# Squared-ReLU MLP: first layer by one level of Strassen's method (Winograd's form), MLP in 4 chunks

## The chip, the cores and the metric

The kernel runs on one core of a Trainium2 chip. The metric is the device time of one execution in microseconds (us); the figure quoted for a kernel is the median of several executions. Engines are named as in the profile: PE is TensorE, PEld its weight loads, DVE is VectorE, ACT is ScalarE, POOL is GpSimd, SP issues most DMA.

## What is computed

One layer of a streaming encoder on 512 tokens (S) of width 1024 (D):

```
h = rmsnorm(x); [u|v|bg|cg|xs|ga|gb] = h @ w_in          # 1024 x 7168
a = gelu(u) * (blockwise spatial gating of rmsnorm(gelu(v)))
c = bg * causal_conv3(cg * xs)
m = sigmoid(ga) * (a @ w_proj_a) + sigmoid(gb) * (c @ w_proj_b)
x = x + m @ w_out
z = relu(rmsnorm(x) @ w_ff1)                             # 1024 x 4096
x = x + (z * z) @ w_ff2                                  # 4096 x 1024
y = rmsnorm(x)
```

All data is float32. The change is to the two MLP products (the last three lines but one), and to the weight stream that all of the products share.

## The kernel before

Channels lie on the 128 partitions and tokens on the free axis. Every float32 operand is split into hi + lo, both in the type float32r, and a product is three TensorE matmuls: hi*hi, hi*lo, lo*hi (lines 120 to 122).

The weight stream comes in **units** of 1024 x 128 weights (512 KB). `prep` (line 97) loads a unit into a `raw` tile (4 of them) through SP's queue, rounds it to `whi` on ACT (line 84) and subtracts to get `wlo` on DVE (line 85); `wsp` holds 3 pairs of whi and wlo, and preparation runs two units ahead. `unit_matmuls` (line 110) then issues 8 k tiles x 3 = 24 matmuls of 128 x 128 weights on 512 tokens into one PSUM bank.

The MLP runs in 2 chunks (`NCH = 2`), each with 16 tiles of 128 of the 4096 inner channels. In a chunk the first layer takes 16 units; each bank goes through `z_evac` (line 365): max(.,0) times the token's rstd on DVE (`t_z`, line 367), the square on ACT (`q`, line 369), and a split into zh and zl (lines 84, 85). Then for each of the 8 output tiles the second layer takes two units (48 matmuls into one bank), and DVE adds the bank to `res` (line 475). The norm's statistic for the first layer (`rstd_of`, `spread`) is worked out while the first two tiles run. The very last output tile (`last_tile`, line 409) is done by halves of 256 tokens, in 96 matmuls of 256 columns (lines 424 to 426), so that the final norm of the first half runs beside the second.

Each engine works in the order of its own instruction list, which the tile framework's scheduler writes; an instruction that waits holds up what is behind it on its engine.

Of the kernel before, what the change touches and what calls it, by code (L numbers as in the profile page):

```python
# [31 lines left out]
def hybrid_block(ctx, tc, xT, vecs, w_v, w_main, w_s, b_s, out_a, out_b):  # L32
# [12 lines left out]
    outp = ctx.enter_context(tc.tile_pool(name="outp", bufs=4))  # L45
# [19 lines left out]
    # TensorE reaches its full clock while the first loads are under way.  # L65
# [15 lines left out]
    def split_into(hi, lo, src, scale=None):  # L81
        """hi + lo = src (or src * scale), each part rounded to float32r."""
# [12 lines left out]
    parts = {}  # L95

    def prep(i):
        if i >= n_units or i in parts:
            return
        r = raws.tile([P, KT * P], F32, name="raw")  # L100
        nc.sync.dma_start(r, w_main[i])
        hi = wsp.tile([P, KT * P], F32R, name="whi")
        lo = wsp.tile([P, KT * P], F32R, name="wlo")
        split_into(hi, lo, r)
        parts[i] = (hi, lo)

    state = {"next": 0}
    AHEAD = 2

    def unit_matmuls(psum, act_hi, act_lo, start=True, stop=True, cols=slice(0, S)):  # L110
        """psum += W_unit.T @ act over the unit's 8 k tiles."""
        i = state["next"]
        state["next"] += 1
        prep(i)
        for a in range(1, AHEAD + 1):
            prep(i + a)
        hi, lo = parts.pop(i)
        for k in range(KT):
            ks = slice(k * P, (k + 1) * P)
            nc.tensor.matmul(psum, hi[:, ks], act_hi[k][:, cols], start=start and k == 0, stop=False)  # L120
            nc.tensor.matmul(psum, hi[:, ks], act_lo[k][:, cols], start=False, stop=False)  # L121
            nc.tensor.matmul(psum, lo[:, ks], act_hi[k][:, cols], start=False, stop=stop and k == KT - 1)  # L122
# [23 lines left out]
    def spread(r, n=NB):  # L146
        """rstd as [token, block] -> [any partition, token], in PSUM."""
# [10 lines left out]
    xh = [shared("X", 16, f"xh{k}", F32R) for k in range(KT)]  # L158
    xl = [shared("X", 16, f"xl{k}", F32R) for k in range(KT)]
    acc = shared("acc", 1, "acc")  # L160
    vt = [[shared("V", 8, f"vt{b}{h}") for h in range(2)] for b in range(NB)]
    wsT = [shared("M", 16, f"wsT{i}").rearrange("p (g i) -> p g i", i=P) for i in range(2)]
    bsb = [shared("M", 16, f"bsb{i}").rearrange("p (g i) -> p g i", i=P) for i in range(2)]
    vsum = small.tile([P, 2, NB], F32, name="vsum")

    vparts = {}

    def prep_v(i):
        if i >= 2 * KT:
            prep(i - 2 * KT)  # L170
# [4 lines left out]
        t = raws.tile([P, KT * P], F32, name="raw")[:, :HALF]  # L175
        nc.sync.dma_start(t, w_v[h, k])
        vh = shared("M", 16, f"vh{h}{k}", F32R)
        vl = shared("M", 16, f"vl{h}{k}", F32R)
# [30 lines left out]
    for i in range(2 * KT):  # L209
# [330 lines left out]
```

## Time and profile before

| | |
|---|---|
| median of 3 executions | 813.45 us (813.43 to 813.47) |
| profiled execution, first to last instruction (span) | 811.9 us |
| PE busy | 804.2 us (99%), 3646 matmuls |
| PEld busy | 667.2 us (82%) |
| DVE busy | 376.0 us (46%) |
| ACT busy | 250.6 us (31%) |
| DMA | 81.35 MB, mean 100 GB/s |

The profile gives the span of the profiled execution and no other time of it; the median of the timed runs lies 1.55 us above that span. The share of busy time is an average over stages, and a busy PE is not a PE at its peak, since matmuls overlap in the records: how fast it works is read from the starts of successive matmuls. An engine's idle time counts only where another waits for it.

### The profile page before, as it was taken

Reading aid. Unit: us, or ns where it says so; the run is one execution under the profiler, and the core shown is the slowest. Engines: PE = TensorE matmul, PEld = TensorE weight load, DVE = VectorE, ACT = ScalarE, POOL = GpSimd, SP = SyncE. Lnnn points to the kernel's source line nnn. Section 1 sums busy time; section 2 is a strip of 40 time slices with the busy share of each in tenths; the row PEclk is TensorE's granted clock in tenths of the full one; section 3 lists DMA queues with packets and bytes.
Section 4 is the critical chain, followed back from the end, with each engine's and each line's share of the span. In section 5 each row is a group of like instructions: output and inputs, shape, how many; then the busy total and the mean of one; then the engine's idle time right before and its main releaser. Section 6 shows DMA issues by size and latency. Waiting matters only on the chain.

```text
span 811.9 us, 8874 instructions
## 1 busy us (share of the span) xinstructions
PE 804.2 (99%) x3646; PEld 667.2 (82%) x3646; DVE 376.0 (46%) x501; ACT 250.6 (31%) x324; POOL 6.1 (1%) x15
## 2 busy tenths in 40 slices
PE   9999999999999999999999999999999999999996
PEld 6888888888888888888888888888888888888886
DVE  7555653334555555444455554442233445434433
ACT  7323332222212222332344253332112334422221
POOL 0000000000000000000000000000000000000000
PEclk9999999999999999999999999999999999999998
DMA  7522223322332233233223223223322332233203
GB/s 247 195 105 104 78 77 105 104 90 92 104 104 82 100 105 103 79 104 103 93 89 105 97 84 105 101 81 104 103 93 89 105 103 85 97 104 104 79 0 105
DMA packets 25352, 81.35 MB, mean 100 GB/s; under 512 B 2768, under 2 KB 3792, under 8 KB 25312
## 3 DMA queue, kind: packets, MB, share of 16 engines
q1 hardware_dynamic: 24416, 79.18, 29.1%
q10 hardware_dynamic: 864, 1.57, 0.6%
q8 instruction: 28, 0.46, 0.3%
q14 instruction: 12, 0.10, 0.0%
q0 software_dynamic: 32, 0.03, 0.0%
HBM read 78.68 MB, written 2.10 MB: 99 GB/s over the span
## 4 chain that ended last, share of the span: by engine, by line
PE 98%; DMA 0%; ACT 0%; DVEq 0%; POOLq 0%; POOL 0%; DVE 0%; issue 0%
PE bank L121 30%; PE bank L120 30%; PE bank L122 30%; PE bank L219 5%; PE bank L270 1%; PE bank L425 0%; PE bank L426 0%; PE bank L424 0%; DMA res<-xT 0%; PE bank L152 0%; PE st L141 0%; DVEq L534 0%; PE bank L393 0%; PE st L441 0%; POOLq L534 0%; ACT xh L87 0%
## 5 line engine op out<-in xcount | busy, mean ns | idle before, releaser
L84 ACT CAST whi<-raw 128x1024 fp32r<-128x1024 f32 x136 | 143.4, 1054 | 494.2 <-PE bank L121 373.9
L85 DVE TENSOR_TENSOR wlo<-raw,whi 128x1024 fp32r<-128x1024 f32 x136 | 166.5, 1225 | 78.7 <-ACT whi L84 77.6
L120 PE MATMUL bank<-xh,whi 128*128 128x512 f32 x384 | 150.0, 391 | 0.0
L121 PE MATMUL bank<-xl,whi 128*128 128x512 f32 x384 | 149.4, 389 | 0.0
L122 PE MATMUL bank<-xh,wlo 128*128 128x512 f32 x384 | 149.4, 389 | 0.0
L120 PE MATMUL bank<-x2h,whi 128*128 128x512 f32 x256 | 99.8, 390 | 0.0
L122 PE MATMUL bank<-x2h,wlo 128*128 128x512 f32 x256 | 99.6, 389 | 0.0
L121 PE MATMUL bank<-x2l,whi 128*128 128x512 f32 x256 | 99.6, 389 | 0.0
L120 PE MATMUL bank<-zh,whi 128*128 128x512 f32 x240 | 93.4, 389 | 0.0
L121 PE MATMUL bank<-zl,whi 128*128 128x512 f32 x240 | 93.4, 389 | 0.0
L122 PE MATMUL bank<-zh,wlo 128*128 128x512 f32 x240 | 93.4, 389 | 0.0
L122 PEld LDWEIGHTS bank<-xh,wlo 128*128 128x128 f32 x384 | 72.1, 188 | 15.0
L120 PEld LDWEIGHTS bank<-xh,whi 128*128 128x128 f32 x384 | 72.2, 188 | 14.8
L121 PEld LDWEIGHTS bank<-xl,whi 128*128 128x128 f32 x384 | 72.1, 188 | 14.6
L367 DVE SCALAR_TENSOR_TENSOR t_z<-bank,Rf 128x512 f32<-128x512 f32 x32 | 22.0, 691 | 78.8 <-PE bank L122 78.8
L121 PEld LDWEIGHTS bank<-x2l,whi 128*128 128x128 f32 x256 | 48.1, 188 | 10.0
L122 PEld LDWEIGHTS bank<-x2h,wlo 128*128 128x128 f32 x256 | 48.1, 188 | 10.0
L120 PEld LDWEIGHTS bank<-x2h,whi 128*128 128x128 f32 x256 | 48.1, 188 | 9.9
L121 PEld LDWEIGHTS bank<-zl,whi 128*128 128x128 f32 x240 | 45.1, 188 | 9.4
L122 PEld LDWEIGHTS bank<-zh,wlo 128*128 128x128 f32 x240 | 45.1, 188 | 9.3
L120 PEld LDWEIGHTS bank<-zh,whi 128*128 128x128 f32 x240 | 45.1, 188 | 9.3
L475 DVE TENSOR_TENSOR res<-bank,res 128x512 f32<-128x512 f32 x15 | 10.4, 692 | 50.1 <-PE bank L122 50.1
(118 smaller groups left out, 818.6 us busy)
## 6 DMA issues: line engine op xcount, KB each, us to landing
raw<-w_main SPq DMA_DIRECT2D x136, 512.0 KB, 3.2
raw<-w_v SPq DMA_DIRECT2D x16, 256.0 KB, 4.0
res<-xT SPq DMA_DIRECT2D x8, 256.5 KB, 4.8
out_a<-o SPq DMA_DIRECT2D x4, 256.0 KB, 2.4
wsT<-w_sT ACTq DMA_DIRECT2D x2, 256.0 KB, 5.0
bsb<-b_sb ACTq DMA_DIRECT2D x2, 256.0 KB, 5.5
out_b<-ob ACTq DMA_DIRECT2D x2, 256.0 KB, 3.0
out_b<-ob SPq DMA_DIRECT2D x2, 256.0 KB, 3.1
```

Source lines behind the costliest of these rows:

```text
L84: nc.scalar.copy(hi, src)
L85: nc.vector.tensor_tensor(lo, src, hi.bitcast(F32), op=ALU.subtract)
L120: nc.tensor.matmul(psum, hi[:, ks], act_hi[k][:, cols], start=start and k == 0, stop=False)
L121: nc.tensor.matmul(psum, hi[:, ks], act_lo[k][:, cols], start=False, stop=False)
L122: nc.tensor.matmul(psum, lo[:, ks], act_hi[k][:, cols], start=False, stop=stop and k == KT - 1)
L219: nc.tensor.matmul(vbanks[h][b], xs[k][:, b * P : (b + 1) * P], ws, start=k == 0 and ws is vh and xs is xh, stop=k == KT - 1 and xs is xl,)
L270: nc.tensor.matmul(pm[:, b * P : (b + 1) * P], vt[b][g // 4][:, (g % 4) * P : (g % 4 + 1) * P], wsT[g // 4][:, g % 4, :], start=True, stop ...
L367: nc.vector.scalar_tensor_tensor(t, pz, 0.0, Rf, op0=ALU.max, op1=ALU.mult)
L475: nc.vector.tensor_add(res[j], py, res[j])
```

## The change

**Strassen.** The first layer is computed for two output tiles (a **pair**, 256 inner channels) at a time, as a 2 x 2 block product: the 1024 x 256 weights are cut into four blocks of 512 x 128, and the activations into four of 512 x 256 (two halves of the channels by two halves of the tokens). Winograd's form of Strassen's method needs 7 block products (P1, P2, D, F, P6, E, P7) instead of 8; each is 4 k tiles x 3 = 12 matmuls of 256 columns. Left operands are weight blocks or sums of them, right operands activation blocks or sums of them.

- The activation sums are made once, by `combos`, while the output projection runs (its tiles are taken in the order 0, 4, 1, 5, ... so that the blocks that belong together are ready together).
- The weight sums are made per pair on DVE: `add1` (one instruction of 1024 elements per partition) and `add2` (two of 512). A pair then has four operands to split on ACT and DVE: t0 (two raw blocks), t1 (one raw block, 512 elements), t2 and t3 (two sums each).
- The products are gathered in three PSUM banks and put together on ACT (three copies of 256) and DVE (five instructions of 256) into the two output tiles c1 and c2, on which `z_evac` now works. P7 of a pair is issued behind P2 of the next pair (`flush_late`). P6 and P7 go on accumulating in the half bank A, after what stood there has been read.

**Chunks.** `NCH` is 4: 4 pairs, then 8 units of the second layer (24 matmuls each), four times; one pair of the next chunk is computed ahead (5, 4, 4 and 3 pairs). The last two output tiles instead of the last one are done by halves of the tokens, with 8 k tiles each.

**Weight stream.** `raw` tiles are 1 MB (two units, or a pair's four blocks), and there are 2. `whi`/`wlo` is a ring of 4 operands; an operand is prepared when the one four places before is done. v's weights have tiles of their own.

The core of the diff:

```diff
-NCH = 2
+NCH = 4
+RING = 4
-    raws = ctx.enter_context(tc.tile_pool(name="raws", bufs=4))
-    wsp = ctx.enter_context(tc.tile_pool(name="wsp", bufs=3))
+    raws = ctx.enter_context(tc.tile_pool(name="raws", bufs=2))
+    wsp = ctx.enter_context(tc.tile_pool(name="wsp", bufs=RING))
...
+            def add1(raw=raw, sm=sm):
+                nc.vector.tensor_tensor(
+                    sm[0], raw(1, 3), raw(3, 4).broadcast_to([P, 2, S]), op=ALU.add
+                )
+            def add2(raw=raw, sm=sm, key=key):
+                nc.vector.tensor_tensor(sm[1][:, 1, :], sm[0][:, 1, :], raw(1, 2)[:, 0, :], op=ALU.add)
+                nc.vector.tensor_tensor(sm[1][:, 0, :], sm[1][:, 1, :], raw(0, 1)[:, 0, :], op=ALU.add)
+                load_after(key)
+            tl = []
+            tl.append(add_operand(lambda raw=raw: raw(0, 2)))
+            steps.append((add1, None))
+            tl.append(add_operand(lambda raw=raw: raw(2, 3), n=1))
+            steps.append((add2, None))
+            tl.append(add_operand(lambda sm=sm: sm[1]))
+            tl.append(add_operand(lambda sm=sm: sm[0]))
...
+    LEFT = {"P1": (0, 1, "B11"), "P2": (0, 0, "B21"), "D": (1, 0, "nT4"), "F": (2, 0, "B22"),
+            "P6": (2, 1, "nT2"), "E": (3, 1, "nT1"), "P7": (3, 0, "T3")}
+    def product(p, name, out, first, last=False):
+        t, g, r = LEFT[name]
+        o = pairs[p][t]
+        pump()
+        need(o)
+        for sl in range(KS):
+            c = slice(sl * P, (sl + 1) * P)
+            w_hi, w_lo = o["hi"][:, g, c], o["lo"][:, g, c]
+            x_hi, x_lo = right[r, sl, 0], right[r, sl, 1]
+            nc.tensor.matmul(out, w_hi, x_hi, start=first and sl == 0, stop=False, skip_group_check=True)
+            nc.tensor.matmul(out, w_hi, x_lo, start=False, stop=False, skip_group_check=True)
+            nc.tensor.matmul(out, w_lo, x_hi, start=False, stop=sl == KS - 1, skip_group_check=True)
+        if name in ("P2", "D", "P6", "P7"):
+            o["done"] = True
...
+    def block_pair(p, after):
+        ba, bf, bd = bank(), bank(), bank()
+        A, P2 = ba[:, :N2], ba[:, N2:]
+        F = bf[:, :N2]
+        Dp, E = bd[:, :N2], bd[:, N2:]
+        c1, c2 = temp("c1"), temp("c2")
+        product(p, "P1", A, True)
+        product(p, "P2", P2, False)
+        nc.scalar.copy(c1[:, :N2], A)
+        nc.vector.tensor_add(c1[:, :N2], P2, c1[:, :N2])
+        flush_late()
+        product(p, "D", Dp, True)
+        product(p, "F", F, True)
+        product(p, "P6", A, False)
+        nc.scalar.copy(c1[:, N2:], A)
+        nc.vector.tensor_add(c1[:, N2:], F, c1[:, N2:])
+        product(p, "E", E, False)
+        def end():
+            product(p, "P7", A, False)
+            nc.vector.tensor_add(c1[:, N2:], E, c1[:, N2:])
+            nc.scalar.copy(c2[:, :N2], A)
+            nc.vector.scalar_tensor_tensor(c2[:, N2:], E, -1.0, c2[:, :N2], op0=ALU.mult, op1=ALU.subtract)
+            nc.vector.tensor_sub(c2[:, :N2], Dp, c2[:, :N2])
+            after(c1, c2)
+        late.append(end)
...
     for ck in range(NCH):
-        for i in range(CF):
-            pz = bank()
-            unit_matmuls(pz, xh2, xl2)
...
+        end = min((ck + 1) * CF // 2 + 1, NP1)
+        for p in range(done, end):
+            ff1_pair(p)
+        done = end
+        flush_late()
...
-                unit_matmuls(py, zh[0:8], zl[0:8], stop=False)
-                unit_matmuls(py, zh[8:16], zl[8:16], start=False)
+            unit_matmuls(py, zh, zl)
```

How the instruction lists change is shown at two places. The first is PE in the first layer. Before, a tile is 24 matmuls of 512 columns; these are the first six of the fourth tile (x2h, x2l are the activations' hi and lo):

```order
L120 MATMUL bank_3436<-x2h0_2961,whi_3348 128x512
L121 MATMUL bank_3436<-x2l0_2969,whi_3348 128x512
L122 MATMUL bank_3436<-x2h0_2961,wlo_3349 128x512
L120 MATMUL bank_3436<-x2h1_2962,whi_3348 128x512
L121 MATMUL bank_3436<-x2l1_2970,whi_3348 128x512
L122 MATMUL bank_3436<-x2h1_2962,wlo_3349 128x512
```

Now the same engine in the changed kernel, at the end of P2 of the third pair (bank_3448, operand 3393) and the start of the late P7 of the second pair (bank_3322, operand 3377); `cmb` and `cmv` tiles hold the activations' blocks and sums:

```order
L493 MATMUL bank_3448<-cmv1_2842,whi_3393 128x256
L494 MATMUL bank_3448<-cmv1_2842,whi_3393 128x256
L495 MATMUL bank_3448<-cmv1_2842,wlo_3394 128x256
L493 MATMUL bank_3322<-cmb1_2834,whi_3377 128x256 [waits Activation_49]
L494 MATMUL bank_3322<-cmb1_2834,whi_3377 128x256
L495 MATMUL bank_3322<-cmb1_2834,wlo_3378 128x256
```

A pair has 84 such matmuls of 256 columns in place of 48 of 512, and P7 now stands between P2 and D of the pair behind, with a wait for ACT's copy out of the half bank that it goes on filling.

The second place is DVE in the steady part of the first layer. Before, a tile takes three instructions; here are two tiles:

```order
L367 SCALAR_TENSOR_TENSOR t_z_3430<-bank_3399,Rf_3272 128x512
L85 TENSOR_TENSOR wlo_3440<-raw_3437,whi_3439 128x1024
L85 TENSOR_TENSOR zl0_2_3291<-q_3432,zh0_2_3275 128x512
L367 SCALAR_TENSOR_TENSOR t_z_3467<-bank_3436,Rf_3272 128x512
L85 TENSOR_TENSOR wlo_3477<-raw_3474,whi_3476 128x1024
L85 TENSOR_TENSOR zl0_3_3292<-q_3469,zh0_3_3276 128x512
```

Now a whole round of DVE's list in the changed kernel, in two pieces that follow on each other: from the split of t3 of the third pair (from wsum0) to that of t3 of the fourth (from wsum2). Third pair: bank_3448 and 3449, 3450, c1_3451; second pair: bank_3324, c1_3325, c2_3326; raw_3329 is the fourth pair's weights, raw_3455 the fifth's.

```order
L96 TENSOR_TENSOR wlo_3512<-wsum0_2847,whi_3511 128x1024
L515 TENSOR_TENSOR c1_3451<-bank_3448,c1_3451 128x256
L528 SCALAR_TENSOR_TENSOR c2_3326<-bank_3324,c2_3326 128x256
L96 TENSOR_TENSOR zm0_3192<-c1_3325,zm0_3192 128x512
L529 TENSOR_TENSOR c2_3326<-bank_3324,c2_3326 128x256
L96 TENSOR_TENSOR wlo_3528<-raw_3329,whi_3527 128x1024
L576 SCALAR_TENSOR_TENSOR c2_3326<-c2_3326,Rf_3189 128x512
L96 TENSOR_TENSOR wlo_3559<-raw_3329,whi_3558 128x512
```

This first piece splits t3, t0 and t1 and finishes c2 of the second pair; the second piece is:

```order
L467 TENSOR_TENSOR wsum3_2850<-wsum3_2850,raw_3329 128x512
L521 TENSOR_TENSOR c1_3451<-bank_3449,c1_3451 128x256
L96 TENSOR_TENSOR zm1_3193<-c2_3326,zm1_3193 128x512
L526 TENSOR_TENSOR c1_3451<-bank_3450,c1_3451 128x256
L96 TENSOR_TENSOR wlo_3596<-wsum3_2850,whi_3595 128x1024
L576 SCALAR_TENSOR_TENSOR c1_3451<-c1_3451,Rf_3189 128x512
L460 TENSOR_TENSOR wsum0_2847<-raw_3455 128x1024
L96 TENSOR_TENSOR wlo_3638<-wsum2_2849,whi_3637 128x1024
```

A pair now takes 15 DVE instructions in a round in place of 6, and the first combining instruction of a pair (L515), behind which P6 waits, stands behind the split of that pair's t3.

## Rows read from the trace of the kernel before

**Rows 1.** Cores: span and mean granted TensorE clock.

```profile
core 0: 811.9 us, clock 0.997
```

**Rows 2.** Windows: stretch, length, busy time (instructions) of each engine, granted clock, DMA.

```profile
50.50:456.00 405.50, 405.50 (x1828) 336.92 (x1826) 205.59 (x268) 117.08 (x142) 1.01 (x1) 1.00 0.28 94
...
458.50:630.00 171.50, 171.50 (x763) 142.16 (x762) 67.20 (x76) 51.36 (x63) 0.00 (x0) 1.00 0.29 96
630.00:789.00 159.00, 159.00 (x703) 131.72 (x702) 66.93 (x83) 52.78 (x73) 0.00 (x0) 1.00 0.26 86
```

**Rows 3.** The chain that ended last, shares by engine.

```profile
PE 98%; DMA 0%; ACT 0%; DVEq 0%; POOLq 0%; POOL 0%; DVE 0%; issue 0%
```

**Rows 4.** Timeline of PE, first layer: start, length, matmul of 512 columns.

```profile
500.79 0.39 PE L121 MATMUL bank<-x2l,whi 128*128 128x512 f32 x1
...
503.96 0.39 PE L120 MATMUL bank<-x2h,whi 128*128 128x512 f32 x1
```

**Rows 5.** Timeline of PE, last output tile: matmuls of 256 columns.

```profile
789.56 0.28 PE L424 MATMUL bank<-zh,whi 128*128 128x256 f32 x1
789.68 0.28 PE L425 MATMUL bank<-zl,whi 128*128 128x256 f32 x1
...
796.28 0.28 PE L426 MATMUL bank<-zh,wlo 128*128 128x256 f32 x1
```

**Rows 6.** Groups by form: count, busy us, mean ns, idle before.

```profile
L85 DVE TENSOR_TENSOR wlo<-raw,whi 128x1024 fp32r<-128x1024 f32 x136 | 166.5, 1225 | 78.7 <-ACT whi L84 77.6
L84 ACT CAST whi<-raw 128x1024 fp32r<-128x1024 f32 x136 | 143.4, 1054 | 494.2 <-PE bank L121 373.9 <-issue 113.1 <-DMA raw<-w_main 7.3
...
L369 ACT ACTIVATE q<-t_z 128x512 f32<-128x512 f32 x32 | 20.0, 626 | 2.7 <-DVE t_z L367 2.6
L84 ACT CAST zh<-q 128x512 fp32r<-128x512 f32 x32 | 19.9, 622 | 1.0
...
L424 PEld LDWEIGHTS bank<-zh,whi 128*128 128x128 f32 x32 | 6.1, 191 | 0.0
...
L87 ACT ACTIVATE x2h<-res,vec 128x512 fp32r<-128x512 f32 x8 | 5.7, 718 | 0.0
...
L192 DVE TENSOR_TENSOR accb<-accb,sq 128x512 f32<-128x512 f32 x7 | 4.8, 685 | 0.0
```

**Rows 7.** Timeline of DVE, first layer: start, length, and in brackets idle before.

```profile
501.44 0.69 DVE L367 SCALAR_TENSOR_TENSOR t_z<-bank,Rf 128x512 f32<-128x512 f32 x1 [2.70 <-PE bank L122]
502.31 1.22 DVE L85 TENSOR_TENSOR wlo<-raw,whi 128x1024 fp32r<-128x1024 f32 x1 [0.17 <-ACT whi L84]
503.49 0.69 DVE L85 TENSOR_TENSOR zl<-q,zh 128x512 fp32r<-128x512 f32 x1
506.88 0.69 DVE L367 SCALAR_TENSOR_TENSOR t_z<-bank,Rf 128x512 f32<-128x512 f32 x1 [2.70 <-PE bank L122]
```

**Rows 8.** Timeline of DVE: instructions that follow on each other without a wait.

```profile
35.36 0.69 DVE L199 SCALAR_TENSOR_TENSOR sq<-vt 128x512 f32<-128x512 f32 x1
...
35.97 0.69 DVE L199 SCALAR_TENSOR_TENSOR sq<-vt 128x512 f32<-128x512 f32 x1
...
255.62 1.23 DVE L85 TENSOR_TENSOR wlo<-raw,whi 128x1024 fp32r<-128x1024 f32 x1 [0.17 <-ACT whi L84]
256.77 0.69 DVE L85 TENSOR_TENSOR cl<-c,ch 128x512 fp32r<-128x512 f32 x1
...
799.45 2.74 DVE L383 TENSOR_TENSOR o<-res,bank 128x256 f32<-128x256 f32 x8 [0.61 <-PE bank L152]
```

**Rows 9.** Timeline, all engines: from the last tile's last matmul on.

```profile
802.71 0.28 PE L426 MATMUL bank<-zh,wlo 128*128 128x256 f32 x1
...
803.03 0.42 DVE L429 TENSOR_TENSOR res<-bank,res 128x256 f32<-128x256 f32 x1 [0.85 <-PE bank L426]
803.49 0.42 ACT L431 ACTIVATE sq<-res 128x256 f32<-128x256 f32 x1 [7.09 <-DVE res L429]
```

**Rows 10.** DMA issues: count, KB each, median us from issue to landing.

```profile
raw<-w_main SPq DMA_DIRECT2D x136, 512.0 KB, 3.2
```

More of the change, by code (lines that the diff above doesn't have):

```diff
@@ L94, in hybrid_block @@
     n_units = w_main.shape[0]
-    parts = {}
-    def prep(i):
-        if i >= n_units or i in parts:
-            return
[L100 to L105, printed above, removed]
-    state = {"next": 0}
[L108 to L122, printed above, removed]
+    steps = []
@@ new lines, in hybrid_block, with load, load_after @@
+    opnds = []
+    raw_of = {}
+    def load(key):
+        if key in raw_of:
+            return
+        r = raws.tile([P, 4, S], F32, name="raw")
+        kind, i = key
+        if kind == "u":
+            nc.sync.dma_start(
+                r.rearrange("p (u a) s -> p u (a s)", u=2), w_main[i : i + 2].rearrange("u p f -> p u f")
+            )
+        else:
+            nc.sync.dma_start(r, w_ff1[i])
+        raw_of[key] = r
+    loads = []
+    def load_after(key):
+        n = loads.index(key) + 2
+        if n < len(loads):
+            load(loads[n])
@@ new lines, in add_operand, with step @@
+    def add_operand(src, n=2, last=None):
+        o = {"done": False, "ready": False, "idx": len(opnds)}
+        def step():
+            hi = wsp.tile([P, n, S], F32R, name="whi", padded_shape=[P, 2, S])
+            lo = wsp.tile([P, n, S], F32R, name="wlo", padded_shape=[P, 2, S])
+            split_into(hi, lo, src())
+            o["hi"], o["lo"], o["ready"] = hi, lo, True
+            if last:
+                load_after(last)
+        opnds.append(o)
+        steps.append((step, o))
+        return o
@@ new lines, in pump, with need, plan_units @@
+    def pump(n=1):
+        while steps and n:
+            step, o = steps[0]
+            if o is not None and o["idx"] >= RING and not opnds[o["idx"] - RING]["done"]:
+                return
+            steps.pop(0)
+            step()
+            n -= 1
+    def need(o):
+        while not o["ready"]:
+            steps.pop(0)[0]()
+    units = []
+    def plan_units(n):
+        for _ in range(n // 2):
+            i = len(units)
+            key = ("u", i)
+            loads.append(key)
+            for e in range(2):
+                units.append(add_operand(
+                    lambda key=key, e=e: raw_of[key][:, 2 * e : 2 * e + 2, :], last=key if e else None
+                ))
@@ new lines, in hybrid_block, with unit_matmuls @@
+    state = {"next": 0}
+    def unit_matmuls(psum, act_hi, act_lo, start=True, stop=True, cols=slice(0, S), ks=range(KT), o=None):
+        if o is None:
+            o = units[state["next"]]
+            state["next"] += 1
+            pump()
+            need(o)
+            o["done"] = True
+        hi, lo = (o[h].rearrange("p a s -> p (a s)") for h in ("hi", "lo"))
+        for k in ks:
+            c = slice(k * P, (k + 1) * P)
+            first, end = start and k == 0, stop and k == KT - 1
+            nc.tensor.matmul(psum, hi[:, c], act_hi[k][:, cols], start=first, stop=False)
+            nc.tensor.matmul(psum, hi[:, c], act_lo[k][:, cols], start=False, stop=False)
+            nc.tensor.matmul(psum, lo[:, c], act_hi[k][:, cols], start=False, stop=end)
@@ L174, in prep_v @@
             nc.sync.dma_start(resg[k], xT[k])
[L175 removed]
+        if i % 2 == 0:
+            vraw.append(wide("AC", f"vraw{i}"))
+        t = vraw[-1][:, i % 2, :]
         nc.sync.dma_start(t, w_v[h, k])
[L177 to L178 removed]
+        if i == 2 * KT - 1:
+            for key in loads[:2]:
+                load(key)
+        vp = wide("M", f"vp{h}{k}", F32R)
+        vh, vl = vp[:, 0, :], vp[:, 1, :]
         if h == 0:
@@ new lines, in hybrid_block @@
+    LEFT = {"P1": (0, 1, "B11"), "P2": (0, 0, "B21"), "D": (1, 0, "nT4"), "F": (2, 0, "B22"),
[3 more added lines that the diff above has]
+        o = pairs[p][t]
+        pump()
+        need(o)
+        for sl in range(KS):
+            c = slice(sl * P, (sl + 1) * P)
[5 more added lines that the diff above has]
+        if name in ("P2", "D", "P6", "P7"):
+            o["done"] = True
@@ new lines, in hybrid_block, with flush_late @@
+    late = []
+    def flush_late():
+        while late:
+            late.pop(0)()
+    def block_pair(p, after):
[23 more added lines that the diff above has]
+        late.append(end)
@@ L352, in hybrid_block @@
+    plan_pairs(CF // 2 + 1)
+    for ck in range(NCH):
+        plan_units(KT)
+        if ck < NCH - 1:
+            plan_pairs(CF // 2 - (ck == NCH - 2))
     acc = shared("acc", 1, "accb")
-    for j in range(KT):
+    xg = {}
+    for n in range(KT):
+        j = n // 2 + 4 * (n % 2)
         po = bank()
@@ L407, in finish_second, with last_tiles @@
                 eng.dma_start(out_b[n, :, h * HALF : (h + 1) * HALF], o)
-    def last_tile(j):
-        i0 = state["next"]
-        state["next"] += 2
-        prep(i0)
-        prep(i0 + 1)
+    def last_tiles(js):
+        us = units[state["next"] : state["next"] + len(js)]
+        state["next"] += len(js)
+        for o in us:
+            need(o)
         todo = []
```

198 lines of the change are left out of this document (123 added, 75 removed).

## The prediction

> **What bounds the kernel now.** First the cores and the windows: the one core runs at a granted clock of 0.997 over a span of 811.9 us, and in the windows from 50.5 us to 789 us PE is busy all the time, with a clock of 1.00 [rows 1, 2]. The chain that ended last says the same: 98% of it is PE [rows 3]. A busy PE is not yet a PE that can't go faster, so next the starts of its matmuls. In the first layer of the MLP they are 14 steps in 3.17 us apart, 0.2264 us each for 512 columns [rows 4]; 24 of them are 5.44 us, which is also the time from one tile's evacuation to the next on DVE [rows 7], so the waits at a unit's start cost nothing. PE's pace is that of its matmuls, and everything else hides: in the 171.5 us window around the first MLP chunk DVE is busy for 67.2 us and ACT for 51.4 [rows 2].
>
> So a time comes out of two questions: how much PE work goes, and whether DVE and ACT, which get more of it, still hide.
>
> **PE's work.** The same kernel shows the size that the change uses: the last output tile runs in matmuls of 256 columns, 56 steps in 6.72 us, 0.1200 us each, though every one has a weight load of 191 ns beside it [rows 5, 6]. A matmul of 512 costs less than two of 256 (0.2264 against 0.2400), by about 0.0136 us that each matmul has on top of its columns. A pair of tiles cost 48 x 0.2264 = 10.87 us and will cost 84 x 0.1200 = 10.08: 0.79 us less, 7.3% and not the 12.5% that 7 products for 8 promise. For 16 pairs that is 12.6 us. The rest of PE's work stays: the second layer has 720 matmuls of 512 (15 tiles of 48 before, 30 groups of 24 after) and 96 of 256. (The Trainium skill, TensorE: Matmul & The Clock Gate, section Back-to-back issue gap, gives N/2.4 + 2.5 ns for a warm gap: 215.8 and 109.2 ns. By that the pair would go from 10.36 to 9.17 us, and 19.0 us would be gained. The rows have a longer gap at both sizes, and they decide.)
>
> **DVE's work.** What a DVE instruction takes from the queue is the distance to the next start, which is shorter than its recorded length: 0.61 us for 512 elements of 0.69, 1.15 for 1024 of 1.23, and 8 of 256 elements run in 2.74, so 0.33 each [rows 8]. Sums of two SBUF tiles are no slower than splits (685 ns for accb, [rows 6]), so I take the weight sums at these prices; a broadcast operand is not in the trace, and I take it at the same price (if it cost double, add1 would add 1.15 us to a round). A round of the first chunk, as the order lists it, is then: 4 instructions of 1024 (three splits, add1) 4.6; 6 of 512 (two z splits, two evacuations, one short split, half of add2) 3.66; 5 of 256 (the combining) 1.67. Together 9.9 us, against 10.08 of PE. Before, a pair took 2 x (1.23 + 0.69 + 0.69) = 5.2. So DVE goes from half loaded to 98% in a round of chunk 0. In the later chunks part of the sums falls into the second layer (where DVE has 1.15 + 0.61 per 5.44 us and much room), and by the same count their rounds are 5.1, 9.4 and 9.3 us: room of 0.7 us or more. ACT has three casts of 1054 ns and a short one, two z casts and two squares at 622 to 626 [rows 6], and three copies of about 0.42 [rows 9]: 3.8 + 2.5 + 1.3 = 7.6 us per pair, which fits.
>
> **The tight loop.** A ring of 4 operands lets DVE work ahead only so far, and one chain goes round through three engines. P7 of the last pair holds t3's place; when it is done, ACT casts t3 of this pair, DVE splits it, then DVE does L515, then P6 may write into the half bank. Behind P7 PE has D and F, 24 x 0.120 = 2.88 us. The chain: 0.20 from the end of the last matmul's slot (802.83) to a consumer's start, then 1.05, a handoff of 0.04 (803.45 to 803.49), 1.15 of DVE, 0.42 for L515, 0.05 back to PE [rows 5, 6, 8, 9]: 2.91. Cover and chain are equal, so any delay in it shows on PE. I take 0.1 us for the 11 or 12 pairs where DVE has room, and 0.3 us for four of chunk 0, where DVE arrives at t3 with about 0.2 us to spare: 1.2 + 1.2 = 2.4 us. From below it could be nothing.
>
> **Start and end of the first layer.** The activation sums run while PE does the output projection. DVE has 8.2 us there per two tiles (two residual adds, five 256 instructions, three splits, two accb, two weight splits) for 10.9 us of PE. Exposed is only what hangs on the last tile: the add to res (0.69), the scaled copy (0.72) and a cast (0.62) are 2.3 us with what lies between, and PE has P1 and three quarters of P2, 21 x 0.12 = 2.5 us, meanwhile. The last sum, nT4, comes later, since ACT must first cast t3 (it waits for the last tile's end) and t0 of the second pair: about 6.9 us after that end, where PE, with P1, P2, F, three quarters of D and the statistic, arrives at about 6.5. I put 0.4 us. In the last chunk the second layer starts on the pair just computed: z of its c2 is ready about 6.5 us after P7, and PE, which takes parts of two units first, gets there at about 6.4: 0.2 us.
>
> **The weight stream.** Loads are 1 MB instead of 512 KB; those took 3.2 us [rows 10], so at most 6.4. A pair's load is issued when the t1 split two pairs ahead has let the raw tile go, some 10 us or more before its first reader: hidden. If it were not, add1 would be late, and with it DVE's whole round.
>
> **The sum.** -12.6 + 2.4 + 0.4 + 0.2 = -9.6 us on a span of 811.9, so 802.3; the median of the runs lies 1.55 above the span, which gives 803.9 us.
>
> **Rivals.**
> - DVE becomes the bound of the first layer. If the recorded lengths counted in full, a round of chunk 0 would be 4 x 1.23 + 6 x 0.69 + 5 x 0.42 = 11.2 us, 1.1 above PE, and the rounds of 9.3 to 9.4 would be 10.5, 0.4 above: 4 x 1.1 + 6 x 0.4 = 6.8 us lost in place of the 2.4, so 808.3 us. Against it: in the trace independent instructions start 80 ns early [rows 8], and the list puts another instruction between most dependent ones. For it: nearly every instruction there waits for another engine, and the count leaves no room for that. (The Trainium skill, VectorE: DVE Perf Modes, section The DRAIN you can't avoid, says that the next operation does not start until the pipe is empty; by that this would be the case. The rows show starts before the recorded end, so the trace doesn't bear it out in full.)
> - Slower than before: the tight loop. Each pair pays what L515 is late at P6. If one more instruction of 1024 came between on DVE or on ACT, because the engine is behind when P7 ends, every pair would lose 1.15 us, 18.4 in all, and the kernel would need 813.45 - 12.6 + 18.4 + 0.6 = 819.9 us. It turns to a loss from 0.75 us per pair on. For it: cover and chain are equal, 2.88 against 2.91. Against: outside chunk 0 DVE has 0.7 us or more to spare in a round, and such a delay isn't carried on.
> - Near no change: about 11 us lost in waits, by both of these in part. Between 812 and 815 us.
> - The short gap between matmuls of 256 holds only in the last tile, and is better elsewhere. By the page's gap named above it would be 813.45 - 19.0 + 3.0 = 797.5 us; nothing in the rows shows such a gap.
>
> **How the numbers follow.** 0.2% of the time, 1.6 us, is about what a measurement of this kernel can tell from no change. The forecast, PE still the bound and small waits, 801 to 806 us: 0.65. DVE as the bound, 806 to 811.8: 0.20. Near no change: 0.05. Slower, the loop: 0.08. The shorter gap: 0.02. So faster 0.87, same 0.05, slower 0.08. The range must hold 8 in 10: all of the forecast's cases and most of the second rival's, from no waits at all (813.45 - 12.6 = 800.85, a little less for the start of the kernel) to 809.5. It goes 800.3 to 809.5.
>
> **What the profile would show.** Right: in the first layer 256-column matmuls 0.120 us apart, PE busy for over 97% of a chunk's first layer, a pair in 10.1 to 10.5 us; waits of PE mainly at the first matmul of P6 (for DVE) and in the first pair; DVE busy nine tenths and more. Wrong: gaps of 0.5 us or more in every pair in front of P6, E or P1 (loop or DVE as the bound, told apart by whether DVE is idle before t3's split); gaps in the output projection; add1 waiting for a load; or another pitch than 0.120.

## The result, and the profile after

The changed kernel takes 802.65 us (median of 4 executions, 802.61 to 803.3) against 813.46 for the kernel before on the same chip: ratio 0.9866, 95% interval [0.9854, 0.9879]. The forecast was 803.9, range 800.3 to 809.5, faster. Run again later, the same kernel took 802.61 against 813.56, ratio 0.9864 [0.985, 0.9877].

The cores view answers to [rows 1]: 11.2 us less span, and no loss of clock.

```profile
core 0: 800.7 us, clock 0.998
```

The windows answer to [rows 2]; the columns are those of that group. The first row is the first layer of chunk 0 (from the norm's statistic on), the second mostly the second layer of that chunk, the third most of the first layer of chunk 1.

```profile
456.00:506.00 50.00, 49.62 (x400) 48.83 (x400) 47.50 (x77) 30.03 (x49) 2.46 (x1) 1.00 0.30 106
506.00:550.00 44.00, 44.00 (x209) 36.98 (x209) 23.43 (x28) 10.73 (x13) 0.00 (x0) 1.00 0.27 96
550.00:590.00 40.00, 40.00 (x322) 39.18 (x321) 35.16 (x53) 24.93 (x42) 0.00 (x0) 1.00 0.32 106
```

PE is still busy all the time, but for 0.38 us in the first row, a wait at the statistic. DVE went from 67.2 of 171.5 us to 47.50 of 50 in chunk 0 (95%), 35.16 of 40 in chunk 1 and 23.43 of 44 in the second layer. The chain's shares by engine, to be held against [rows 3], say the same: 98% PE again, with 1% of DVE as the only newcomer.

```profile
PE 98%; DVE 1%; DMA 0%; ACT 0%; POOLq 0%; DVEq 0%; issue 0%
```

PE's timeline shows a steady pair, the third: its first matmul (P1, tile `b`), the first of the next pair's P1, and the pitch; it answers to [rows 5].

```profile
471.30 0.28 PE L493 MATMUL bank<-b,whi 128*128 128x256 f32 x1
471.42 0.28 PE L494 MATMUL bank<-b,whi 128*128 128x256 f32 x1
...
481.38 0.28 PE L493 MATMUL bank<-b,whi 128*128 128x256 f32 x1
481.50 0.28 PE L494 MATMUL bank<-b,whi 128*128 128x256 f32 x1
```

From 471.30 to 481.38 are 10.08 us: 84 matmuls of 0.1200 us, with no wait at all. All steady pairs are like that (a later one starts at 565.48, the next at 575.56).

The groups by form answer to [rows 6]. Splits and casts kept their lengths, the sum with the broadcast operand (L460) is as long as a split, and the short sums are 0.69 us as taken.

```profile
L96 DVE TENSOR_TENSOR wlo<-raw,whi 128x1024 fp32r<-128x1024 f32 x120 | 146.7, 1222 | 13.6 <-ACT whi L95 13.0
L95 ACT CAST whi<-raw 128x1024 fp32r<-128x1024 f32 x120 | 125.9, 1054 | 329.1 <-PE bank L190 289.5 <-issue 19.3 <-PE bank L494 14.7
...
L460 DVE TENSOR_TENSOR wsum<-raw 128x1024 f32<-128x1024 f32 x16 | 19.5, 1219 | 0.1
...
L466 DVE TENSOR_TENSOR wsum<-wsum,raw 128x512 f32<-128x512 f32 x16 | 11.0, 688 | 0.3
...
L515 DVE TENSOR_TENSOR c<-bank,c 128x256 f32<-128x256 f32 x16 | 6.7, 418 | 0.0
```

The DMA issues answer to [rows 10]: 1 MB lands in 4.9 us, inside the 6.4 that the forecast allowed, and nothing in the MLP waits for a load.

```profile
raw<-w_main SPq DMA_DIRECT2D x52, 1024.0 KB, 4.9
raw<-w_ff SPq DMA_DIRECT2D x16, 1024.0 KB, 4.7
```

**Where the time came from.** From the first matmul of the MLP to its last, before took from 450.40 to 802.83, and after from 449.95 to 791.35: 352.43 and 341.40 us, so 11.0 of the 11.2 us were gained there. The matmuls alone give 12.6. What is missing, some 1.6 us, are waits of PE. Summed up to the two last tiles, the distances of matmul starts beyond the pitch come to 1.7 us, and 0.6 us more stand between the small matmuls of the norm's statistic and what follows on them; in the kernel before both together are 0.2 us. They are all at edges: at the norm's statistic in the first layer, at P6 of the first pair of chunks 1 to 3, at P7 of the last pair of each chunk, and at the last chunk's z. Against them the matmuls of the two last tiles wait 0.2 us, where those of the one last tile waited 0.6. The remaining 0.2 us of the span are the 0.45 us by which the MLP starts earlier, less 0.2 us that the tail behind it is longer.

### The profile page after: what moved, and what is told of

Same layout as the page of the kernel before. It is cut to its first block, busy times and chain, and to the rows that moved or that the text cites. A ratio compares the mean times of both kernels' runs of the same rounds, so it can differ in the third digit from the quotient of the medians.

```text
span 800.7 us, 10145 instructions
## 1 busy us (share of the span) xinstructions
PE 792.6 (99%) x4222; PEld 684.2 (85%) x4222; DVE 485.4 (61%) x702; ACT 293.6 (37%) x420; POOL 7.6 (1%) x15
## 4 chain that ended last, share of the span: by engine, by line
PE 98%; DVE 1%; DMA 0%; ACT 0%; POOLq 0%; DVEq 0%; issue 0%
PE bank L190 24%; PE bank L189 24%; PE bank L191 24%; PE bank L493 7%; PE bank L494 7%; PE bank L495 6%; PE bank L302 5%; PE bank L351 1%; DMA res<-xT 0%; PE bank L221 0%; DVE wlo L96 0%; PE bank L600 0%; DVE cmv L96 0%; PE st L646 0%; PE st L210 0%; DVE ob L612 0%
## 5 line engine op out<-in xcount | busy, mean ns | idle before, releaser
L95 ACT CAST whi<-raw 128x1024 fp32r<-128x1024 f32 (+1 forms) x136 | 135.2, 1003 | 347.0 <-PE bank L190 305.4
L96 DVE TENSOR_TENSOR wlo<-raw,whi 128x1024 fp32r<-128x1024 f32 (+1 forms) x136 | 157.5, 1159 | 13.6 <-ACT whi L95 13.0
L189 PE MATMUL bank<-x,whi 128*128 128x512 f32 x384 | 150.0, 391 | 0.0
L190 PE MATMUL bank<-x,whi 128*128 128x512 f32 x384 | 149.4, 389 | 0.0
L191 PE MATMUL bank<-x,wlo 128*128 128x512 f32 x384 | 149.4, 389 | 0.0
L190 PEld LDWEIGHTS bank<-x,whi 128*128 128x128 f32 x384 | 72.1, 188 | 14.8
L189 PEld LDWEIGHTS bank<-x,whi 128*128 128x128 f32 x384 | 72.1, 188 | 14.8
L189 PE MATMUL bank<-zm,whi 128*128 128x512 f32 (+1 forms) x204 | 77.0, 378 | 0.0
L191 PE MATMUL bank<-zm,wlo 128*128 128x512 f32 (+1 forms) x204 | 76.9, 377 | 0.0
L190 PE MATMUL bank<-zm,whi 128*128 128x512 f32 (+1 forms) x204 | 76.8, 377 | 0.0
L493 PE MATMUL bank<-cmb,whi 128*128 128x256 f32 x256 | 73.1, 286 | 0.0
L495 PE MATMUL bank<-cmb,wlo 128*128 128x256 f32 x256 | 72.4, 283 | 0.0
L494 PE MATMUL bank<-cmb,whi 128*128 128x256 f32 x256 | 72.4, 283 | 0.0
L493 PEld LDWEIGHTS bank<-cmb,whi 128*128 128x128 f32 x256 | 49.1, 192 | 1.3 <-ACT c L520 1.0
L494 PEld LDWEIGHTS bank<-cmb,whi 128*128 128x128 f32 x256 | 49.1, 192 | 0.0
L495 PEld LDWEIGHTS bank<-cmb,wlo 128*128 128x128 f32 x256 | 49.1, 192 | 0.0
```

What stands on the lines that cost most here:

```text
L95: nc.scalar.copy(hi, src)
L96: nc.vector.tensor_tensor(lo, src, hi.bitcast(F32), op=ALU.subtract)
L189: nc.tensor.matmul(psum, hi[:, c], act_hi[k][:, cols], start=first, stop=False)
L190: nc.tensor.matmul(psum, hi[:, c], act_lo[k][:, cols], start=False, stop=False)
L191: nc.tensor.matmul(psum, lo[:, c], act_hi[k][:, cols], start=False, stop=end)
L493: nc.tensor.matmul(out, w_hi, x_hi, start=first and sl == 0, stop=False, skip_group_check=True)
```

## The experiments

The theory was: PE's pitch sets the time, the gain is 16 times 0.79 us, and the extra DVE work hides in the steady pairs. Its rival was that DVE, or the loop through PE, ACT and DVE, costs something in every pair. The first four kernels ran on one chip (the kernel before there: 813.71 us), the next four on another (813.56), and the last one beside 813.61; a difference between runs of different chips carries up to some 0.25 us of that.

**Everything but Strassen.** The first layer is back to plain tiles of 512 columns; four chunks, 1 MB loads, the ring of operands, the new order of the output projection and two last tiles by halves stay.

```diff
...
-        for p in range(done, end):
-            ff1_pair(p)
...
+        for i in range(ck * CF, (ck + 1) * CF):
+            pz = bank()
+            unit_matmuls(pz, x2h, x2l)
...
```

> All of the change but Strassen: 4 chunks, 1 MB loads, ring of 4, the new order of the output projection, the last two tiles by halves; the first layer is 32 tiles of 24 matmuls of 512 columns as before. Theory (the gain is PE's shorter first layer, 16 x 0.79 us, and nothing else of weight): the gain goes, 812.5 to 813.5 us, about 0.4 us of it kept from an earlier start of the MLP (449.95 against 450.40 us in the two traces). Rival (the gain is from the weight stream or the four chunks): stays near 803 us.

Measured: 813.45 us, ratio 0.9996 [0.9987, 1.0005]. The other parts of the change together are worth nothing that can be told (0.26 us), and the gain is Strassen's.

**Plain tiles in halves of 256 columns.** As above, with each tile in two halves: 96 matmuls of 256 in place of 48 of 512 per pair.

```diff
-            unit_matmuls(pz, x2h, x2l)
+            for hf in range(2):
+                cs = slice(hf * N2, (hf + 1) * N2)
...
+                unit_matmuls(pz[:, cs], x2h, x2l, cols=cs, o=o)
```

> As e1, but every first-layer tile in two halves of 256 tokens: 8 block products' worth of 256-column matmuls, 96 per pair in place of 84, without sums. Theory (a matmul of 256 takes 0.120 us wherever it stands, 0.0136 of it on top of half a matmul of 512): a pair takes 11.52 us against 10.87, so 16 x 0.65 = 10.4 us above e1, 823 to 824 us. Rival (the extra 0.0136 us belongs to the last tile only): within 2 us of e1.

Measured: 823.87 us, ratio 1.0124 [1.0109, 1.0139], 10.42 us above the run before it. 16 x (96 x 0.1200 - 48 x 0.2264) is 10.4. So the fixed 0.0136 us of each matmul is paid in the whole first layer, and it is what Strassen's method loses here: 7 products for 8 would be 12.5% of a pair, and are 7.3%.

**No weight sums.** Only add1 and add2 go: this kernel leaves out the sums, and splits t2 and t3 from raw blocks in their place.

```diff
-            steps.append((add1, None))
...
-            steps.append((add2, None))
-            tl.append(add_operand(lambda sm=sm: sm[1]))
-            tl.append(add_operand(lambda sm=sm: sm[0]))
+            tl.append(add_operand(lambda raw=raw: raw(1, 3)))
+            tl.append(add_operand(lambda raw=raw: raw(2, 4), last=key))
```

> Leaves out the weight sums (t2 and t3 are split from raw blocks instead of sums), so DVE has 2.36 us less per pair (about 23%). Theory (DVE hides even at 95% busy, PE is paced by its matmuls): 802.0 to 802.8 us, at most 0.6 us less. Rival (DVE's load costs PE waits throughout the first layer): 800.8 to 801.6 us, since about 1.8 us of waits stand in the MLP.

Measured: 801.22 us, ratio 0.9846 [0.9831, 0.986], 1.4 us below the changed kernel in time and 1.0 in span. That is the rival's number, but the place is not the rival's. A steady pair had no wait to give back; what went are the waits at the chunk edges. They are too short for the profile's list of waits, which in both kernels shows only the 0.4 us at the statistic; the distances beyond the pitch show them, and these sum to 0.5 us here and to 1.7 in the changed kernel. So the 2.4 us of sums that DVE does for each of 16 pairs cost 1.0 to 1.4 us in all.

**One sum of 1024 elements twice.**

```diff
                 nc.vector.tensor_tensor(
                     sm[0], raw(1, 3), raw(3, 4).broadcast_to([P, 2, S]), op=ALU.add
                 )
+                nc.vector.tensor_tensor(
+                    sm[0], raw(1, 3), raw(3, 4).broadcast_to([P, 2, S]), op=ALU.add
+                )
```

> add1 is done twice: one more DVE instruction of 1024 elements (1.15 us) per pair. Theory (DVE's rounds are 9.9 us of 10.08 in the first chunk and 9.3 in the others, so they have next to no room): in the first chunk three rounds grow to 11.05 us and cost PE about 1.0 us each, in the other chunks the sums fall partly into the second layer and one round of each grows to 10.5, 0.4 us: 804.5 to 807 us. Rival (lookahead of the ring and the room in other rounds absorb it): below 803.3 us.

Measured: 804.51 us, ratio 0.9888 [0.9871, 0.9904], 1.9 us more than the changed kernel in time and in span. PE's timeline shows the new waits in two pairs of chunk 0 only; this is the second (L496 is L493 of the changed kernel):

```profile
498.14 0.28 PE L498 MATMUL bank<-cmv,wlo 128*128 128x256 f32 x1
499.04 0.39 PE L496 MATMUL bank<-cmb,whi 128*128 128x256 f32 x1 [0.62 <-ACT whi L95]
```

0.90 us between two starts in place of 0.12. The earlier rounds of chunk 0 still passed without such a wait, on what DVE had worked ahead, and the other chunks gained no wait at all; the one at P6 of their first pair even went. The time is at the low end of the theory's, but the theory had 0.4 us in each of the other chunks too.

**The changed kernel again,** on the chip of the runs that follow.

> The changed kernel as it is, beside the three that follow, so that these are compared with it on one chip. Both theories: 802.0 to 803.3 us, ratio to the kernel before 0.9855 to 0.9880. What the three are to tell apart. Theory A: DVE's load costs nothing in the steady pairs (they are 10.08 us apart without a wait) and shows only at the edges of the chunks, where a short instruction that PE needs stands behind a long one. Theory B: the loop through PE, ACT and DVE is on the edge in every pair, and each addition to it or relief of it shows in most of the 16 pairs.

Measured: 802.61 us, ratio 0.9864 [0.985, 0.9877], span 800.7.

**P7 at once.** The late part of a pair runs right behind E.

```diff
-        late.append(end)
+        end()
```

> P7 of every pair runs right behind its E, not behind P1 and P2 of the next pair. This gives the loop (end of P7, cast of t3, split of t3, L515, P6) two products more of cover, and takes cover from L520, which P7 waits for: only E, 12 x 0.120 = 1.44 us, is then in front of it, as at the last pair of each chunk now, where P7 waits some 0.17 us. Theory A: the loop costs nothing in the steady pairs, so nothing comes back there, and the wait of P7 comes in up to 12 more pairs: +0.3 to +2 us, 803.0 to 804.7. Theory B: the loop's relief pays more than that: 801.0 to 802.3.

Measured: 804.16 us, ratio 0.9882 [0.9868, 0.9895]; 1.55 us more. Theory A. In PE's timeline 14 of the 16 first matmuls of P7 now take 0.22 us to the next start in place of 0.12, and three of them also start 0.13 to 0.15 us late. This is one of the three:

```profile
491.54 0.28 PE L495 MATMUL bank<-cmv,wlo 128*128 128x256 f32 x1
491.80 0.38 PE L493 MATMUL bank<-cmb,whi 128*128 128x256 f32 x1
```

and on ACT the copy that it waits for ends just in front of it:

```profile
491.38 0.37 ACT L520 COPY c<-bank 128x256 f32<-128x256 f32 x1 [1.97 <-PE bank L495]
```

The copy ends at 491.75, P7 starts at 491.80, 0.14 us late, and the second matmul comes 0.22 us behind the first, 0.10 us more than the pitch: 0.25 us for this pair. The other eleven start less than 0.02 us late and lose the 0.10 alone; four P7 at the chunks' ends had lost that in the changed kernel too. So the late P7 of the change is worth 1.5 us.

**The sums on GpSimd.**

```diff
-                nc.vector.tensor_tensor(
+                nc.gpsimd.tensor_tensor(
                     sm[0], raw(1, 3), raw(3, 4).broadcast_to([P, 2, S]), op=ALU.add
                 )
...
-                nc.vector.tensor_tensor(sm[1][:, 1, :], sm[0][:, 1, :], raw(1, 2)[:, 0, :], op=ALU.add)
-                nc.vector.tensor_tensor(sm[1][:, 0, :], sm[1][:, 1, :], raw(0, 1)[:, 0, :], op=ALU.add)
+                nc.gpsimd.tensor_tensor(sm[1][:, 1, :], sm[0][:, 1, :], raw(1, 2)[:, 0, :], op=ALU.add)
+                nc.gpsimd.tensor_tensor(sm[1][:, 0, :], sm[1][:, 1, :], raw(0, 1)[:, 0, :], op=ALU.add)
```

> The three sums of weight blocks of each pair run on GpSimd instead of DVE, the same result. DVE's round of chunk 0 falls from 9.9 us by 1.15 + 2 x 0.61 to 7.5. How long GpSimd needs for 128 x 1024 the traces so far do not show (it does 128 x 4 only). Theory A: as long as GpSimd ends its 2048 columns within the 10.08 us of a pair and DVE keeps its durations, the waits at the chunk edges go as they did when the sums were left out: 801.0 to 801.8 us. Rival: GpSimd is slow enough that t2 and t3 come late, or it slows DVE beside it; then PE waits in front of P6 and E in every pair, and with 0.5 us per pair the time is 810 us or more.

Measured: 813.59 us, ratio 1.0003 [0.9994, 1.0011]: the whole gain is gone. The rival, and by its second half, though PE does not wait in every pair. The groups of POOL show what the sums take there:

```profile
L460 POOL TENSOR_TENSOR wsum<-raw 128x1024 f32<-128x1024 f32 x16 | 40.0, 2500 | 579.5 <-DVE res L559 369.2 <-DMA raw<-w_ff 147.5 <-DVE wlo L96 62.8
L467 POOL TENSOR_TENSOR wsum<-wsum,raw 128x512 f32<-128x512 f32 x16 | 27.2, 1697 | 1.2
L466 POOL TENSOR_TENSOR wsum<-wsum,raw 128x512 f32<-128x512 f32 x16 | 25.4, 1591 | 1.2
```

5.8 us per pair, which is well inside 10.08. But DVE stops meanwhile. Its timeline at the start of the first layer:

```profile
453.63 2.86 DVE L96 TENSOR_TENSOR cmv<-xg,cmv 128x512 fp32r<-128x512 f32 x1
456.41 1.51 DVE L542 SCALAR_TENSOR_TENSOR nT2nT<-nT1T,xg 128x256 f32<-128x256 f32 x1
457.84 1.77 DVE L96 TENSOR_TENSOR cmv<-nT1T,cmv 128x512 fp32r<-128x512 f32 x1
459.53 0.41 DVE L543 TENSOR_TENSOR nT2nT<-nT2nT,xg 128x256 f32<-128x256 f32 x1
```

beside that of POOL:

```profile
453.46 2.48 POOL L460 TENSOR_TENSOR wsum<-raw 128x1024 f32<-128x1024 f32 x1 [8.79 <-DVE wlo L96]
456.02 1.62 POOL L466 TENSOR_TENSOR wsum<-wsum,raw 128x512 f32<-128x512 f32 x1
457.72 1.34 POOL L467 TENSOR_TENSOR wsum<-wsum,raw 128x512 f32<-128x512 f32 x1
```

Three sums on POOL, and beside each one DVE instruction that is not done until the sum is: 2.86 us for a split that takes 0.69 otherwise, 1.51 for a combination of 256 elements that takes 0.4, 1.77 for the next split. As soon as POOL is idle, the fourth takes 0.41. DVE's combining instructions, which read one operand from PSUM, kept their time beside a sum, while the split behind them did not:

```profile
474.36 2.40 POOL L460 TENSOR_TENSOR wsum<-raw 128x1024 f32<-128x1024 f32 x1 [10.33 <-DVE wlo L96]
```

```profile
474.53 0.41 DVE L528 SCALAR_TENSOR_TENSOR c<-bank,c 128x256 f32<-128x256 f32 x1
474.86 2.45 DVE L96 TENSOR_TENSOR z<-c,z 128x512 fp32r<-128x512 f32 x1
```

PE waits for the first split, and its timeline shows the price:

```profile
454.31 0.28 PE L493 MATMUL bank<-cmv,whi 128*128 128x256 f32 x1
456.54 0.39 PE L494 MATMUL bank<-cmv,whi 128*128 128x256 f32 x1 [1.95 <-DVE cmv L96]
```

A second loss follows from it. The windows before, in and behind the stretch:

```profile
454.00:457.50 3.50, 1.55 (x13) 1.34 (x13) 3.50 (x2) 1.43 (x3) 3.42 (x2) 1.00 0.00 0
457.50:468.00 10.50, 9.36 (x46) 9.07 (x45) 7.45 (x14) 3.33 (x6) 2.50 (x3) 0.51 0.14 51
468.00:506.00 38.00, 36.25 (x301) 35.84 (x300) 35.02 (x45) 21.49 (x36) 12.37 (x6) 1.00 0.27 94
```

PE was busy for 1.55 of 3.50 us, and for the next 10.5 us the granted clock is 0.51, the 1.2 GHz level; matmuls of 256 columns then start 0.213 us apart. P1 of the second pair starts at 468.88 in place of 461.15: 7.7 of the 12.4 us that this execution's span is longer (it is the longest of eleven, 1.6 us above their median); 0.9 of the 7.7 stand ahead of the first matmul of the MLP. The other waits, in front of P6 in chunks 1 to 3 and behind P1's first matmuls in chunks 0 to 2, make up the rest.

(The Trainium skill, SBUF — State Buffer, section Who interferes with whom, says that a DVE instruction with two SBUF inputs contends with a GpSimd instruction that reads SBUF, that the shared pair of ports is an exclusive lock, and that a DVE instruction with at most one SBUF input does not contend. The trace agrees in all three: 2.86 us beside 2.48, none of the three done before its sum, and 0.41 for L528.)

**A sum of 512 elements twice.**

```diff
                 nc.vector.tensor_tensor(sm[1][:, 0, :], sm[1][:, 1, :], raw(0, 1)[:, 0, :], op=ALU.add)
+                nc.vector.tensor_tensor(sm[1][:, 0, :], sm[1][:, 1, :], raw(0, 1)[:, 0, :], op=ALU.add)
```

> The last of the weight sums (512 elements) is done twice, 0.61 us more for DVE per pair. Rounds of chunk 0 go by the predicted count from 9.9 to 10.5 us, 0.4 above PE's 10.08, the others stay at or below 10.0. Theory A: only chunk 0 can lose, and the head start of the ring takes part of it: +0.2 to +1.2 us over the changed kernel, with waits in one or two pairs of chunk 0 (one whole 1024 sum more cost 1.9). Theory B: the 0.61 us come into the loop of nearly every pair: +4 us and more.

Measured: 802.77 us, ratio 0.9866 [0.9851, 0.9881]: 0.16 us above the changed kernel, a hair below the low end of theory A and nothing that can be told from zero. Theory B is out. One new wait stands in chunk 0, of 0.68 us beyond the pitch (L495 and L496 are L494 and L495 of the changed kernel):

```profile
497.24 0.28 PE L495 MATMUL bank<-cmb,whi 128*128 128x256 f32 x1
498.04 0.39 PE L496 MATMUL bank<-cmb,wlo 128*128 128x256 f32 x1 [0.52 <-DVE wlo L96]
```

and about as much went at the norm's statistic, where the list of instructions fell out a little differently.

**The sum of 1024 elements three times.**

```diff
+                nc.vector.tensor_tensor(
+                    sm[0], raw(1, 3), raw(3, 4).broadcast_to([P, 2, S]), op=ALU.add
+                )
+                nc.vector.tensor_tensor(
+                    sm[0], raw(1, 3), raw(3, 4).broadcast_to([P, 2, S]), op=ALU.add
+                )
```

> The first weight sum (1024 elements) is done three times instead of once: 2.3 us more for DVE per pair. By the predicted count the rounds go to 12.2 us in chunk 0 and to 7.4, 11.7 and 11.6 in the other chunks, against PE's 10.08. Theory A (a round costs only what it has above PE's, less what DVE has worked ahead): one sum more gave rounds of 11.05 in chunk 0 and cost 1.9 us where the count alone said 4 x 0.97 = 3.9, so DVE is some 2 us ahead. With two more, chunk 0 loses 4 x 2.1 - 2 = 6.4 us and each later chunk 1.6 + 1.5 less 1 to 2, together 3 to 6: 812 to 815 us. Theory B (the sums stand in the loop of every pair): 16 x 2.3 = 37 us, 839 us.

Measured: 811.87 us (810.79 to 813.2), ratio 0.9979 [0.997, 0.9988], 9.3 us above the changed kernel: theory A had 812 to 815 us, theory B 839. It is next to theory A's sum, but by luck: its parts were not as theory A had them. The windows of chunk 0 and of chunk 1's first layer:

```profile
487.00:491.50 4.50, 1.93 (x15) 1.53 (x14) 4.50 (x9) 1.76 (x4) 0.00 (x0) 1.00 0.05 5
491.50:496.50 5.00, 4.79 (x24) 4.50 (x25) 5.00 (x7) 3.98 (x6) 0.00 (x0) 0.67 0.56 205
...
556.00:598.00 42.00, 42.00 (x344) 41.43 (x343) 38.79 (x55) 24.57 (x39) 0.00 (x0) 1.00 0.21 76
```

In chunk 0 DVE is busy for all of the 4.5 us in which PE works 1.93: DVE is the bound. The clock then falls here too (0.67 over the next 5 us), which theory A had not counted, and once more behind 503.60 to 506.00, where PE works 0.37 of 2.40 us and DVE all of it (0.60 over the next 4.3 us). The later chunks lose nothing: P7 of the last pair of chunk 1 is 10.5 us later than in the changed kernel, that of chunk 3 10.3. So chunk 0 loses some 10 us in this execution, where theory A had 6.4, and the others nothing, where it had 3 to 6. In both kernels DVE does the sums of two of chunk 1's four pairs during the second layer in front of it, and those of the other two in the first layer. What takes the longer sums there is mostly DVE's idle time in the chunk's first round; this is the round from t3's split of the first pair to that of the second, in the changed kernel and here:

```profile
547.69:559.57 11.88, 11.88 (x100) 11.80 (x99) 8.49 (x12) 4.87 (x8) 0.00 (x0) 1.00 0.27 88
...
558.39:570.00 11.61, 11.61 (x100) 11.61 (x98) 10.57 (x13) 4.33 (x7) 0.00 (x0) 1.00 0.25 90
```

3.4 us of idle time became 1.0, and no matmul waited for it. Theory A had counted 1 to 2 us of DVE's lead, and not this room.

## Why the prediction held, step by step

- **PE's pitch and the gain of 12.6 us.** Right to the hundredth: 10.08 us per pair, 10.42 us for the halves where 10.4 was worked out, nothing from the rest of the change. The rival of a shorter gap for 256 columns is out.
- **DVE's round of 9.9 us.** Right in chunk 0: 95% busy over the window where 98% was counted for a round, instructions 80 ns closer than their lengths, and no steady pair held up. The counts for the later chunks (5.1, 9.4 and 9.3 us) were off: from t3's split to t3's split in chunk 1 DVE is busy for 8.49 of 11.88 us, all of 10.75 and 8.19 of 9.28, and PE waits in none but the first. The margin is real but small. 0.6 us more per pair costs nothing that can be told, 1.15 us cost 1.9 in all, 2.3 us cost 9.3. The rival "DVE becomes the bound" is where that last kernel is, and it needed 2.3 us per pair more than the change has.
- **The tight loop, 2.4 us: the step that failed.** The prediction had it that "P7 of the last pair holds t3's place", so that cover and chain were 2.88 and 2.91 us. The trace shows the cast of t3 starting earlier than that. These are PE, ACT and DVE in the third pair: the last matmul of P2, the first of the late P7, and the first of P6,

```profile
474.06 0.28 PE L495 MATMUL bank<-cmv,wlo 128*128 128x256 f32 x1
474.18 0.28 PE L493 MATMUL bank<-cmb,whi 128*128 128x256 f32 x1
...
478.50 0.28 PE L493 MATMUL bank<-cmb,whi 128*128 128x256 f32 x1
```

the cast of t3 on ACT,

```profile
474.26 1.05 ACT L95 CAST whi<-wsum 128x1024 fp32r<-128x1024 f32 x1 [1.33 <-PE bank L494]
```

and on DVE the split and L515:

```profile
475.34 1.23 DVE L96 TENSOR_TENSOR wlo<-wsum,whi 128x1024 fp32r<-128x1024 f32 x1
476.48 0.42 DVE L515 TENSOR_TENSOR c<-bank,c 128x256 f32<-128x256 f32 x1
```

The cast starts when P2 has ended and P7 has only begun. P7 reads the old t3 until 475.62, so the new one can't be in its place; what P2's end gives back is t0, and by this the new t3 stands there (the profile has P2's L494 as what released the cast). So the cover is P7, D and F, 36 x 0.120 = 4.32 us; the chain from 474.18 to the end of L515 at 476.90 is 2.72, near the 2.91 worked out; and 1.6 us are to spare. This fits with a 1024 sum more not costing 1.15 us in each pair, and with nothing gained back when P7 runs at once. In the pair before it the cast starts 0.13 us behind P2's end, in the pair behind it 0.08, and in steady pairs of chunk 1 (568.44, 578.52) 0.08 too; in the last pair of chunk 0 it stands behind other work on ACT and starts at 495.58, still ahead of P7's end at 495.78.
- **Where such a loop was tight after all.** The first pair of chunks 1 to 3 has no late P7 to run behind its P2. Its t3 is split before P2 ends (547.69); what goes round here is t0 of the next pair, which P2's end lets in, and which DVE splits ahead of L515. Its cover is D and F alone, the 2.88 us of the prediction, and half of add2 holds the split up until 0.18 us behind the cast's end, so P6 waits. The cast on ACT, DVE up to L515 and PE around the wait (P2 ends at 549.51):

```profile
549.59 1.05 ACT L95 CAST whi<-raw 128x1024 fp32r<-128x1024 f32 x1 [1.93 <-PE bank L494]
```

```profile
550.21 0.69 DVE L466 TENSOR_TENSOR wsum<-wsum,raw 128x512 f32<-128x512 f32 x1
550.82 1.22 DVE L96 TENSOR_TENSOR wlo<-raw,whi 128x1024 fp32r<-128x1024 f32 x1
551.95 0.42 DVE L515 TENSOR_TENSOR c<-bank,c 128x256 f32<-128x256 f32 x1
```

```profile
552.27 0.28 PE L495 MATMUL bank<-cmv,wlo 128*128 128x256 f32 x1
552.42 0.39 PE L493 MATMUL bank<-cmb,whi 128*128 128x256 f32 x1
552.64 0.28 PE L494 MATMUL bank<-cmb,whi 128*128 128x256 f32 x1
```

0.13 us more than two pitches, three times in all. The other edge, P7 at once at the end of a chunk, costs 0.11 us in chunk 0 and 0.17 to 0.18 each in chunks 1 to 3, and was not forecast. That the waits hang on the sums is shown for both by the kernel without them, which has neither. By one more run it is the place of L515 in DVE's list rather than DVE's load: with the 1024 sum done twice it stands ahead of t0's split there (553.76 against 554.09), and P6 does not wait. How the sums come to delay P7, which waits for a copy on ACT, is not shown.
- **Start and end of the first layer, 0.4 and 0.2 us.** The last sum, nT4, is late as said (0.4 us by the profile), but with what stands around the statistic the start costs some 0.9 us more than before, not 0.4. The last chunk's z costs the 0.2.
- **The sum.** Forecast 802.3 us of span, measured 800.7. The 2.4 us of pair waits were some 1.1 us at the chunk edges instead, which is 1.3 of the 1.6. The rest nearly cancels: the start of the first layer costs 0.5 us more than forecast, and three terms that the sum did not have (0.4 us less of waits in the last tiles, 0.45 us from the earlier start of the MLP, a tail 0.2 us longer) give 0.6 us. That the sum came so near is in part luck, since a wait that is not there stood in it beside others that were priced too low or not at all. The median lies 1.95 us above this span where 1.55 was taken, so the time missed by less, 1.25 us.

## What to carry to other kernels

Price a scheme that saves multiplications with the pitch of the matmuls that it uses, not with its count of products: two fifths of the eighth that the method saves went into the fixed 0.0136 us of smaller matmuls, and the kernel's own timeline had that number in it. When a loop runs through a ring of buffers, find out which release hands the place on before you price it; one product more or less between release and need decided between a wait (the first pair of a chunk) and none (the steady pairs). An engine at 95% in the steady state can cost nothing there and show up at the edges, where the usual cover is missing, so look for the edges; and relief by a second engine is relief only if the two don't hold each other up.

## What the runs showed of the hardware that was not expected

- A sum of two SBUF tiles on GpSimd stops DVE: an instruction of 0.69 us with two SBUF operands took 2.86 beside a GpSimd sum of 2.48, while DVE instructions with an operand in PSUM kept 0.41.
- GpSimd takes 2.50 us in this kernel for the sum of 1024 elements that takes DVE 1.22.
- Behind a stretch in which PE was busy for 1.55 of 3.50 us the granted clock was 0.51 over 10.5 us (the 1.2 GHz level), with matmuls of 256 columns 0.213 us apart; behind one of 1.93 of 4.50 us it was 0.67 as the mean of 5 us. A wait of 1.7 us later in the kernel with sums on GpSimd left the clock at 1.00.
- A PE wait costs more than its gap: at the chunk edges the first matmul behind it takes 0.22 us to the next start in place of 0.12, so a wait of 0.03 us cost 0.13; with P7 at once, eleven P7 that start less than 0.02 us late lose 0.10 us each.
